# The head of a hybrid encoder block: memory loaded in halves, its norm behind the sixth K block, alternating heads, a pad of eight floats

## The chip, the cores and the metric

The kernel runs on one core of a Trainium2 chip, as one program. The metric is the device time of that program in microseconds: the median of several executions. One execution was also taken with the hardware profiler, and its span, from the first to the last instruction, is what the rows below are counted in.

## The reference, cut to what matters

One block of a streaming encoder on x of 512 frames by 1024 channels and a fixed memory of 256 frames by 1024 channels, all in float32. Three sub-layers with RMS norms ahead of them add to x: two recurrent branches that are merged, a cross-attention into the memory, and a gated convolution feed-forward. The change touches three places:

```python
def cross_attention(h, m, w_q, w_kv, w_o):      # m = rms_norm(mem, norm_mem_g)
    kv = m @ w_kv
    k = kv[..., :D_MODEL].reshape(bsz, -1, X_HEADS, X_HEAD_DIM)
    v = kv[..., D_MODEL:].reshape(bsz, -1, X_HEADS, X_HEAD_DIM)
...
def step(state, inp):                            # the first recurrence, 8 heads of 64
    r_t, w_t, k_t, v_t, a_t, b_t = inp
    sa = jnp.einsum('bhij,bhj->bhi', state, a_t)
    state = state * w_t[:, :, None, :] + sa[..., None] * b_t[:, :, None, :] + v_t[..., None] * k_t[:, :, None, :]
    y_t = jnp.einsum('bhij,bhj->bhi', state, r_t)
...
def conv_ffn(h, w_in, conv_w, conv_b, w_out):
    u = h @ w_in
    gate = causal_dwconv(u[..., :D_FF], conv_w, conv_b)
    return (jax.nn.gelu(gate) * u[..., D_FF:]) @ w_out
```

## The kernel before, in words

Every large product is computed as three products of float32r parts: a high part (a copy rounded by ScalarE) and a low part (the difference, by VectorE) of each operand, high by high, high by low, low by high (`mm3`, L163 to L167). `dense` does this for one block of 128 output channels over its blocks of the contraction. Weights come in pieces of 512 KB: the function `stream` loads a piece into one of four raw buffers (`wr`), ScalarE casts it into one of three buffers `wh` (L118), and VectorE subtracts into one of three buffers `wl` (L119). Loads, casts and subtractions have high priority. Each engine works through its own list in order; the order of these lists is laid out before the run by the framework, from the program's order, from priorities and from the times that it expects, so that products of a later part can stand between those of an earlier one. The framework also sets the semaphores.

The run begins with ten matmuls on a constant (`wake`, `NWAKE`). Then keys and values of the memory are computed. The memory is loaded in four quarters of 256 KB (`load_m`) that alternate with the two halves of w_k's first piece on the queue of SP; `split_m` scales one of its eight blocks by the norm's gain and splits it into high and low parts (`m2`). The RMS factor of each memory frame is not applied to the memory but to the results. For that, squares of the raw memory are taken on ScalarE behind the last split (L312, L315) and summed on VectorE (L316), then summed over partitions by TensorE (`rs_ps`, twice more with frames on partitions, `rmc_ps`), and turned into `rm` and `rmc` by Ln and Exp on ScalarE and a Newton step on VectorE (L250 to L254). In the program's order all of that stands ahead of K. The K product has eight blocks of 128 channels; block m needs piece m of w_k, has a PSUM bank of its own (`k_ps`), and is scaled by `rm` on VectorE (`kt`, L335) and written out by a transfer from the queue of POOL. From block 4 on, pieces of x are loaded. The V product follows: two halves of four pieces of w_v each, in PSUM tiles `v_ps`, and between them the sums and the normalisation of x (`x_norm`), which the projection `in_ps` needs.

The first recurrence is worked in eight chunks of 64 frames (`chunk`), at high priority between other matmuls. `rows_v(c)` transposes and centres the values of one chunk by 64x64 products: for each half e of the partitions and each of four pairs j of heads, one product reads the half e and writes the other half of one PSUM bank, 16 instructions in all. The products u read and write the same half; the second products into y (L843) do so too, both halves in one bank, and alternate between the halves.

The feed-forward uses a scheme of seven products (A11, s1, s2, s4, s3, A12, A22) for each pair of blocks of its 22; each has 24 matmuls of 256 columns in a pair, and the order is the one given here. Their moving operands are seven tiles: four in two tiles `hq` of the pool `big`, and three, those of s3, A12 and A22, in the tiles `hr0` to `hr2` of the pool `pr`, which is allocated from the right end of SBUF. The last product's operands `go1` and `go2` have 8 of their 11 blocks in `big` and 3 in the places of hr0 and hr1.

Of the kernel before, what the change touches and what calls it, by code (L numbers as in the profile page):

```python
# [9 lines left out]
F32 = mybir.dt.float32  # L10
F32R = mybir.dt.float32r
AF = mybir.ActivationFunctionType
ALU = mybir.AluOpType
# [4 lines left out]
P = 128  # L18
T = 512
D = 1024  # L20
KB = D // P
NMEM = 256
# [3 lines left out]
NPAIR = NH // 2  # L26
# [5 lines left out]
IN_REST = [22, 23, 24, 25, 26, 27, 28, 29, 30, 31, 32, 33, 34, 35, 36, 37, 14, 15, 16, 17, 18, 19, 20, 21]  # L32
NEARLY = 3
NMID = 10
NWAKE = 10
NPOOL = 2
KVB = 3
IN_ORDER = IN_RWKV + IN_REST
# [19 lines left out]
def hybrid_block_kernel(ctx: ExitStack, tc: tile.TileContext, xT_d, mT_d, pv_d, cst_d, win_d, wk_d, wv_d,  # L58
                        lup_d, gup_d, rga_d, rgx_d, wba_d, wbb_d, wmix_d, wq_d, wo_d, wfi_d, wfo_d, out_d):
    nc = tc.nc  # L60
    V, S, PE = nc.vector, nc.scalar, nc.tensor
# [12 lines left out]
    def mm_ps(name):  # L74
        return pmm.tile([P, T], F32, tag="mm", name=name)

    def rw_ps(name, pool=None, tag="rw", **kw):
        return (pool or prw).tile([P, T], F32, tag=tag, name=name, **kw)
# [15 lines left out]
        return pv[:, o:o + w]  # L94


    wdma, mdma = [], []

    def stream(dram, name, between=None, order=None):

        for g in order or range(dram.shape[0]):
            with tc.high_priority():
                raw = wp.tile([P, 1024], F32, tag="wr", name=f"{name}_r{g}", bufs=4)
                n = 1024 if between is None else 512
                for o in range(0, 1024, n):
                    ins = nc.sync.dma_start(raw[:, o:o + n], dram[g, :, o:o + n])
                    if between is not None:
                        tc.keep_in_program_order(ins)
                        between(o // n)
                    elif len(wdma) == 1:  # L110
                        tc.add_manual_dep(ins.ins, mdma[-1].ins.name, mybir.DependencyInfo(
                            mybir.DependencyClass.NoSync, mybir.DependencyReason.DATA), reason="order of the loads")
                between = None
                wdma.append(ins)
                hi = wp.tile([P, 1024], F32R, tag="wh", name=f"{name}_h{g}")
                lo = wp.tile([P, 1024], F32R, tag="wl", name=f"{name}_l{g}")
                for o in range(0, 1024, n):
                    S.copy(hi[:, o:o + n], raw[:, o:o + n])  # L118
                    V.tensor_tensor(lo[:, o:o + n], raw[:, o:o + n], hi[:, o:o + n].bitcast(F32), ALU.subtract)  # L119
            yield hi, lo  # L120

    def stream_quarters(srcs, name):
# [48 lines left out]
    def sum_behind(ins, n=1):  # L171

        for put in islice(sums, n):
            tc.add_manual_dep(tc.keep_in_program_order(put()).ins, ins.ins.name, mybir.DependencyInfo(
                mybir.DependencyClass.Sync, mybir.DependencyReason.DATA), reason="pace of the sums")

    def dense(ps, units, rhs, nkb, nsum=0):

        for kb in range(nkb):
            wh, wl = units.next()  # L180
            rh, rl = rhs(kb)
            ins = mm3(ps, wh, wl, rh, rl, kb == 0, kb == nkb - 1)
            if kb * nsum % nkb < nsum:
                sum_behind(ins)
        return ins
# [10 lines left out]
    eps = cp.tile([P, 4], F32, name="eps")  # L196
    ones = cp.tile([P, P], F32, name="ones")
# [13 lines left out]
    def rsqrt(out, src, scale, bias, load=True):  # L211

        if load:
            ins = ln_exp_set()
            with tc.issue_after(ins.ins):
                S.activation(out, src, AF.Ln, scale=scale, bias=bias)
                S.activation(out, out, AF.Exp, scale=-0.5)
        else:
            S.activation(out, src, AF.Ln, scale=scale, bias=bias)
            S.activation(out, out, AF.Exp, scale=-0.5)  # L220
# [27 lines left out]
    def newton(y, v, t, scale, bias):  # L248

        V.tensor_scalar(t, v, scale, bias, ALU.mult, ALU.add)  # L250
        V.tensor_tensor(t, t, y, ALU.mult)
        V.tensor_tensor(t, t, y, ALU.mult)
        V.tensor_scalar(t, t, -0.5, 1.5, ALU.mult, ALU.add)
        V.tensor_tensor(y, y, t, ALU.mult)  # L254

    def rstd_bc(out, ssq, n, pool=None, scratch=None, load=True, split=None, **kw):

        ps = rw_ps("rs_ps", pool, **kw)
        if split is None:
            PE.matmul(ps[:, :n], ones, ssq, start=True, stop=True)  # L260
        else:
            sum_exact(ps[:, :n], onesr, ssq, *split)
        rsqrt(out, ps[:, :n], 1.0 / D, eps[:, 0:1], load)
        if scratch is not None:
            newton(out, ps[:, :n], scratch, 1.0 / D, 1e-6)


    dK = dr.tile([KB, P, NMEM], F32, name="dK")
# [3 lines left out]
    with tc.tile_pool(name="p0", bufs=1, reuse_waits="tile") as p0:  # L272
# [6 lines left out]
        o = PV["nmem"][0]  # L279
        tc.keep_in_program_order(nc.scalar.dma_start(gm, pv_d[:, o:o + KB]))  # L280
        ln_exp_set()
        mraw = p0.tile([P, KB, NMEM], F32, name="mraw")
        xraw = p0.tile([P, KB, T], F32, name="xraw")

        def load_m(q):
            with tc.high_priority():
                mdma.append(tc.keep_in_program_order(
                    nc.sync.dma_start(mraw[:, 2 * q:2 * q + 2, :], mT_d[:, 2 * q:2 * q + 2, :])))

        load_m(0)  # L290
        m2 = p0.tile([P, 2, KB, NMEM], F32R, name="m2")

        def split_m(k):
            g = gm[:, k:k + 1]
            hi = S.activation(m2[:, 0, k, :], mraw[:, k, :], AF.Identity, scale=g)
            V.scalar_tensor_tensor(m2[:, 1, k, :], mraw[:, k, :], g, m2[:, 0, k, :].bitcast(F32),
                                   ALU.mult, ALU.subtract)
            return hi

        with tc.high_priority():  # L300
            for k in range(2):
                split_m(k)
        un = Units(wk_d, "wk")
        un.fill(lambda i: [load_m(q) for q in ((1,), (2, 3))[i]])
        tc.keep_in_program_order(nc.scalar.dma_start(pv, pv_d))
        mss = p0.tile([P, NMEM], F32, name="mss")
        msq = [p0.tile([P, NMEM], F32, tag="msq", name=f"msq{k}", bufs=2) for k in range(KB)]
        with tc.high_priority():
            for k in range(2, KB):
                last_m = split_m(k)  # L310
        with tc.issue_after(last_m.ins):
            S.activation(mss, mraw[:, 0, :], AF.Square)  # L312
        for k in range(1, KB):
            with tc.issue_after(last_m.ins):
                S.activation(msq[k], mraw[:, k, :], AF.Square)  # L315
            V.tensor_tensor(mss, mss, msq[k], ALU.add)  # L316
        rm = p0.tile([P, NMEM], F32, name="rm")
        rmt = p0.tile([P, NMEM], F32, name="rmt")
        rstd_bc(rm, mss, NMEM, scratch=rmt)
        rmc = p0.tile([P, 2], F32, name="rmc")  # L320
        psc = rw_ps("rmc_ps")
        for i in range(2):
            PE.matmul(psc[:, i:i + 1], mss[:, i * P:(i + 1) * P], ones[:, 0:1], start=True, stop=True)
        rsqrt(rmc, psc[:, 0:2], 1.0 / D, eps[:, 0:1], load=False)
        newton(rmc, psc[:, 0:2], rmt[:, 0:2], 1.0 / D, 1e-6)


        for m in range(KB):
            ps = rw_ps(f"k_ps{m}") if 3 <= m < 6 else mm_ps(f"k_ps{m}")
            dense(ps[:, :NMEM], un, lambda kb: (m2[:, 0, kb, :], m2[:, 1, kb, :]), KB)  # L330
            if m >= 4:
                with tc.issue_after(wdma[-1].ins):
                    nc.sync.dma_start(xraw[:, 2 * m - 8:2 * m - 6, :], xT_d[:, 2 * m - 8:2 * m - 6, :])
            kt = p0.tile([P, NMEM], F32, tag="kt", name=f"kt{m}", bufs=6)
            last_k = V.tensor_tensor(kt, ps[:, :NMEM], rm, ALU.mult)  # L335
            nc.gpsimd.dma_start(dK[m], kt)
        xss = p0.tile([P, T], F32, name="xss")
        for k in range(KB):
            if k == 0:
# [15 lines left out]
        for hf in range(2):  # L355
            pss = [(mm_ps if hf else rw_ps)(f"v_ps{hf}_{i}") for i in range(2)]
            for k2 in range(4):
                wh, wl = next(st)
                for kk in range(2):
                    kb = 2 * k2 + kk  # L360
# [170 lines left out]
    half = (slice(0, HD), slice(HD, P))  # L531
# [29 lines left out]
    for i in range(2):  # L561
        hs, oh = half[i], half[1 - i]
# [143 lines left out]
    with tc.tile_pool(name="pz", bufs=1, reuse_waits="tile") as pz:  # L706
# [9 lines left out]
        for s in range(30, -1, -1):  # L716
            n = 31 - s
# [66 lines left out]
    def rows_v(c):  # L784

        UV = ch.tile([P, 2, NPAIR, HD], F32, tag="UV", name=f"UV{c}", bufs=2)
        ps = ch_ps(f"vr{c}", "kv")
        for e in range(2):
            hs, oh = half[e], half[1 - e]
            for j in range(NPAIR):  # L790
                PE.matmul(ps[oh, j * HD:(j + 1) * HD], vT[hs, j, c * HD:(c + 1) * HD], centre[hs, hs],
                          start=True, stop=True)
        for e in range(2):
            oh = half[1 - e]
            S.copy(UV[oh, e], j3(ps[oh, 0:256]))
        return UV
# [322 lines left out]
    hq = [big.tile([P, 2, 2, 4, H], F32R, tag=f"act16_{i}", name=f"hq{i}") for i in range(2)]  # L1119
    hop = [hq[0][:, 0], hq[0][:, 1], hq[1][:, 0], hq[1][:, 1]]  # L1120
    hop += [pr.tile([P, 2, 4, H], F32R, tag=f"hr{i}", name=f"hr{i}") for i in range(3)]
    hop = dict(zip(("B11", "b1", "b2", "B22", "b3", "B21", "b4"), hop))
    ssf = cp.tile([P, T], F32, tag="ssq", name="ssf")

# [372 lines left out]
```

## Time and profile before

| | |
|---|---|
| median of 3 runs | 898.03 us (897.56 to 899.0) |
| the profiled execution, its own time | 896.3 us |
| its span, first to last instruction | 894.5 us |
| TensorE busy | 880.9 us, 98% of the span |
| VectorE, ScalarE busy | 686.6 us (77%), 514.8 us (58%) |
| mean granted TensorE clock | 0.997 |

The busy time of TensorE is the union of its instructions; matmuls overlap, so the spacing of their starts says more than the duration of one. Times in rows are in microseconds from the start of the span.

### The profile page before, as it was taken

How to read it: one execution, taken by the hardware profiler on the slowest of the kernel's cores; microseconds unless marked ns; L12 is line 12 of the kernel's file. 1: busy time of each engine (PE TensorE's matmuls, PEld its weight loads, DVE VectorE, ACT ScalarE, POOL GpSimd, SP SyncE). 2: the span in 40 equal slices, each digit the busy share in tenths (PEclk: the TensorE clock that was granted, in tenths of full speed). 3: DMA queues.
4: the chain of work that ended last, by engine and by line, in shares of the span. 5: the costliest groups of instructions: out<-in, count | busy, mean ns of one | idle time of the engine just before them, and what ended most of it. 6: DMA issues, size and time to landing. Idle time of an engine off the chain costs nothing.

```text
span 894.5 us, 15936 instructions
## 1 busy us (share of the span) xinstructions
PE 880.9 (98%) x6196; PEld 771.7 (86%) x6196; DVE 686.6 (77%) x1103; ACT 514.8 (58%) x782; POOL 132.6 (15%) x163
## 2 busy tenths in 40 slices
PE   8999999999999999999999999999999999999996
PEld 6978878888877777888887778999999999999996
DVE  6895598777967677675575578889889888999764
ACT  7665676634347676233554466756655566767553
POOL 0201222021102022001122111111111111202100
PEclk9999999999999999999999999999999999999998
DMA  8878799678987279758888958999989998998963
GB/s 277 292 258 218 202 223 241 184 206 230 266 220 155 73 201 234 230 161 234 217 235 185 196 139 187 256 262 284 260 256 309 256 305 245 259 276 203 282 196 94
DMA packets 97674, 201.37 MB, mean 225 GB/s; under 512 B 19584, under 2 KB 30976, under 8 KB 97536
## 3 DMA queue, kind: packets, MB, share of 16 engines
q1 hardware_dynamic: 62672, 118.57, 40.0%
q0 software_dynamic: 25504, 67.38, 37.0%
q10 hardware_dynamic: 9424, 14.42, 4.7%
q8 instruction: 48, 0.79, 0.4%
q14 instruction: 26, 0.21, 0.1%
HBM read 188.54 MB, written 78.12 MB: 298 GB/s over the span
## 4 chain that ended last, share of the span: by engine, by line
PE 92%; DVE 4%; ACT 1%; issue 1%; DMA 1%; SPq 0%; DVEq 0%; ACTq 0%
PE in_ps L165 7%; PE in_ps L166 7%; PE in_ps L164 7%; PE fx_ps L164 5%; PE fx_ps L165 5%; PE fx_ps L166 5%; PE fyz_ps L165 4%; PE fyz_ps L164 4%; PE fyz_ps L166 3%; PE ox_ps L166 2%; PE ox_ps L164 2%; PE ox_ps L165 2%; PE oyz_ps L166 2%; PE oyz_ps L165 2%; PE oyz_ps L164 2%; PE co_ps L165 2%
## 5 line engine op out<-in xcount | busy, mean ns | idle before, releaser
L130 ACT CAST wfi_h<-wfi_r 128x1024 fp32r<-128x1024 f32 x77 | 81.0, 1052 | 79.9 <-PE fx_ps L165 23.7
L164 PE MATMUL in_ps<-hT,win_h 128*128 128x512 f32 x304 | 120.6, 398 | 0.8 <-ACT hT L351 0.5
L166 PE MATMUL in_ps<-hT,win_l 128*128 128x512 f32 x304 | 121.0, 399 | 0.0
L165 PE MATMUL in_ps<-hT,win_h 128*128 128x512 f32 x304 | 120.9, 399 | 0.1
L131 DVE TENSOR_TENSOR wfi_l<-wfi_r,wfi_h 128x1024 fp32r<-128x1024 f32 x77 | 94.1, 1222 | 23.0 <-ACT wfi_h L130 22.7
L450 POOL DMA_DIRECT2D dS<-in_wfi x66 | 66.7, 1028 | 291.8 <-PE in_ps L164 109.1
L165 PEld LDWEIGHTS in_ps<-hT,win_h 128*128 128x128 f32 x304 | 57.1, 188 | 14.6 <-DVE hT L352 1.1
L164 PEld LDWEIGHTS in_ps<-hT,win_h 128*128 128x128 f32 x304 | 57.0, 188 | 14.3 <-ACT hT L351 1.0
L166 PEld LDWEIGHTS in_ps<-hT,win_l 128*128 128x128 f32 x304 | 57.1, 188 | 12.7 <-issue 0.7
L119 DVE TENSOR_TENSOR win_l<-win_r,win_h 128x1024 fp32r<-128x1024 f32 x38 | 46.3, 1221 | 28.1 <-ACT win_h L118 27.5
L486 POOL DMA_DIRECT2D dOs<-in_wfo x54 | 39.9, 795 | 180.2 <-PE fx_ps L164 50.0
L118 ACT CAST win_h<-win_r 128x1024 fp32r<-128x1024 f32 x38 | 39.9, 1049 | 39.5 <-PE in_ps L165 36.3
L1307 ACT CAST wfo_h<-wfo_r 128x1024 fp32r<-128x1024 f32 (+1 forms) x39 | 40.5, 1038 | 32.0 <-DMA wfo_r<-dOs 10.7
L1308 DVE TENSOR_TENSOR wfo_l<-wfo_r,wfo_h 128x1024 fp32r<-128x1024 f32 (+1 forms) x39 | 47.1, 1208 | 14.1 <-ACT wfo_h L1307 14.0
L164 PE MATMUL fx_ps<-hr,wfi_h 128*128 128x256 f32 x176 | 49.8, 283 | 0.0
L165 PE MATMUL fx_ps<-hr,wfi_h 128*128 128x256 f32 x176 | 49.7, 282 | 0.0
L166 PE MATMUL fx_ps<-hr,wfi_l 128*128 128x256 f32 x176 | 49.3, 280 | 0.0
L164 PE MATMUL fx_ps<-hq,wfi_h 128*128 128x256 f32 x176 | 49.3, 280 | 0.0
L166 PE MATMUL ox_ps<-go,wfo_l 128*128 128x256 f32 x176 | 49.3, 280 | 0.0
L164 PE MATMUL ox_ps<-go,wfo_h 128*128 128x256 f32 x176 | 49.3, 280 | 0.0
L165 PE MATMUL fyz_ps<-hq,wfi_h 128*128 128x256 f32 x176 | 49.3, 280 | 0.0
L165 PE MATMUL fx_ps<-hq,wfi_h 128*128 128x256 f32 x176 | 49.3, 280 | 0.0
(428 smaller groups left out, 2712.2 us busy)
## 6 DMA issues: line engine op xcount, KB each, us to landing
dS<-in_wfi POOLq DMA_DIRECT2D x66, 512.0 KB, 8.0
wfi_r<-dS SPq DMA_DIRECT2D x44, 512.0 KB, 6.5
win_r<-in_win SPq DMA_DIRECT2D x38, 512.0 KB, 5.2
wfi_r<-in_wfi SPq DMA_DIRECT2D x33, 512.0 KB, 5.3
dS<-dS POOLq DMA_DIRECT2D x22, 512.0 KB, 5.5
dOs<-in_wfo POOLq DMA_DIRECT2D x12, 512.0 KB, 8.0
wv_r<-in_wv SPq DMA_DIRECT2D x8, 512.0 KB, 4.9
dG<-gs ACTq DMA_DIRECT2D x16, 256.0 KB, 5.0
```

The source lines that it names most:

```text
L118: S.copy(hi[:, o:o + n], raw[:, o:o + n])
L119: V.tensor_tensor(lo[:, o:o + n], raw[:, o:o + n], hi[:, o:o + n].bitcast(F32), ALU.subtract)
L130: S.copy(hi, raw)
L131: V.tensor_tensor(lo, raw, hi.bitcast(F32), ALU.subtract)
L164: first = PE.matmul(ps, lh, rh, start=start, stop=False, **kw)
L165: PE.matmul(ps, lh, rl, start=False, stop=False, **kw)
L166: PE.matmul(ps, ll, rh, start=False, stop=stop, **kw)
L450: return lambda: nc.gpsimd.dma_start(s(out), src, **kw)
L486: yield lambda k=k, w=w, src=src: nc.gpsimd.dma_start(dO[n, m][:, k * P:(k + w) * P], src, **kw)
L1307: S.copy(hi[:, :n], raw[:, :n])
L1308: V.tensor_tensor(lo[:, :n], raw[:, :n], hi[:, :n].bitcast(F32), ALU.subtract)
```

## The change: what it does

It has three parts. The head of the kernel: the memory is loaded in two halves, w_k's first piece in one transfer between them; the first two pieces of w_k are cast and subtracted in halves; the fourth split of the memory stands between the halves of the first piece; block 1 takes its low products last; the squares stand behind the cast of w_k's third piece; the norm stands behind block 5, and so do the scalings of blocks 0 to 4; two blocks share a PSUM bank, so that six blocks wait for their scaling in three banks; there is an eleventh waking matmul. In `rows_v` the two loops change places. And the pool `pr` gets a fourth tile of eight floats (32 bytes) that nothing uses.

```diff
-NWAKE = 10
+NWAKE = 11
+KNORM = 5
...
                 raw = wp.tile([P, 1024], F32, tag="wr", name=f"{name}_r{g}", bufs=4)
-                n = 1024 if between is None else 512
-                for o in range(0, 1024, n):
-                    ins = nc.sync.dma_start(raw[:, o:o + n], dram[g, :, o:o + n])
...
+                n = 512 if len(wdma) < 2 else 1024
+                ins = nc.sync.dma_start(raw, dram[g])
+                if between is not None:
+                    tc.keep_in_program_order(ins)
+                    between(0)
...
                 for o in range(0, 1024, n):
-                    S.copy(hi[:, o:o + n], raw[:, o:o + n])
+                    casts.append(S.copy(hi[:, o:o + n], raw[:, o:o + n]))
                     V.tensor_tensor(lo[:, o:o + n], raw[:, o:o + n], hi[:, o:o + n].bitcast(F32), ALU.subtract)
+                    if between is not None and o == 0:
+                        between(1)
...
+    def dense_lo_last(ps, units, rhs, nkb):
+
+        w = [units.next() for _ in range(nkb)]
+        for kb in range(nkb):
+            for i in range(2):
+                PE.matmul(ps, w[kb][0], rhs(kb)[i], start=kb == i == 0, stop=False)
+        for kb in range(nkb):
+            PE.matmul(ps, w[kb][1], rhs(kb)[0], start=False, stop=kb == nkb - 1)
...
-                    nc.sync.dma_start(mraw[:, 2 * q:2 * q + 2, :], mT_d[:, 2 * q:2 * q + 2, :])))
+                    nc.sync.dma_start(mraw[:, 4 * q:4 * q + 4, :], mT_d[:, 4 * q:4 * q + 4, :])))
...
-            for k in range(2):
+            for k in range(3):
                 split_m(k)
         un = Units(wk_d, "wk")
-        un.fill(lambda i: [load_m(q) for q in ((1,), (2, 3))[i]])
+        un.fill(lambda i: load_m(1) if i == 0 else split_m(3))
...
+        def m_squares():
+            with tc.issue_after(casts[-1].ins):
+                S.activation(mss, mraw[:, 0, :], AF.Square)
...
+        def m_norm():
+            rstd_bc(rm, mss, NMEM, scratch=rmt)
...
+        def k_out(m):
+            kt = p0.tile([P, NMEM], F32, tag="kt", name=f"kt{m}", bufs=6)
+            ins = V.tensor_tensor(kt, k_ps[m], rm, ALU.mult)
+            nc.gpsimd.dma_start(dK[m], kt)
+            return ins

         for m in range(KB):
-            ps = rw_ps(f"k_ps{m}") if 3 <= m < 6 else mm_ps(f"k_ps{m}")
-            dense(ps[:, :NMEM], un, lambda kb: (m2[:, 0, kb, :], m2[:, 1, kb, :]), KB)
+            if m % 2 == 0:
+                ps2 = (rw_ps if m == 6 else mm_ps)(f"k_ps{m}")
+                k_ps += [ps2[:, :NMEM], ps2[:, NMEM:]]
+            (dense_lo_last if m == 1 else dense)(k_ps[m], un, lambda kb: (m2[:, 0, kb, :], m2[:, 1, kb, :]), KB)
...
+            if m == 2:
+                m_squares()
+            if m == KNORM:
+                m_norm()
+                for i in range(m):
+                    k_out(i)
+            if m >= KNORM:
+                last_k = k_out(m)
...
-        for e in range(2):
-            hs, oh = half[e], half[1 - e]
-            for j in range(NPAIR):
+        for j in range(NPAIR):
+            for e in range(2):
+                hs, oh = half[e], half[1 - e]
                 PE.matmul(ps[oh, j * HD:(j + 1) * HD], vT[hs, j, c * HD:(c + 1) * HD], centre[hs, hs],
                           start=True, stop=True)
...
     hop += [pr.tile([P, 2, 4, H], F32R, tag=f"hr{i}", name=f"hr{i}") for i in range(3)]
+    pr.tile([P, 8], F32, name="pad")
```

## Rows read from the trace of the kernel before

**Rows 1.** The page, first part: busy us, share, instructions of TensorE.
```profile
PE 880.9 (98%) x6196; PEld 771.7 (86%) x6196; DVE 686.6 (77%) x1103; ACT 514.8 (58%) x782; POOL 132.6 (15%) x163
```

**Rows 2.** Waits of TensorE, 5 to 70 us: total, times, longest.
```profile
PE k_ps L166 <- DVE wk_l L119: 1.0, 2, 0.8
...
PE rs_ps L260 <- DVE mss L316: 0.4, 1, 0.4
```

**Rows 3.** Stretches: length, busy of each engine, clock, DMA share, GB/s.
```profile
4.00:6.00 2.00, 2.00 (x7) 1.28 (x5) 1.19 (x3) 1.63 (x4) 0.00 (x0) 1.00 0.94 315
...
8.00:10.00 2.00, 1.28 (x7) 1.00 (x7) 1.26 (x3) 1.82 (x5) 0.00 (x0) 1.00 1.02 412
```

**Rows 4.** Instructions of the memory's tile mraw, durations in ns; its landings.
```profile
L315 ACT ACTIVATE msq<-mraw x7: 400/418/420, 10.2 to 16.8; 128x256 f32<-128x256 f32 x7
...
DMA to landing us min/median/max: 3.3/4.7/6.0
```

**Rows 5.** Timeline of the first microseconds: start, length, engine, line, operation.
```profile
0.75 0.40 SPq L288 DMA_DIRECT2D mraw<-in_mT  x1
...
1.33 4.51 PE L277 MATMUL wake<-onesr 128*128 128x512 f32 x10 [1.33 <-DVE Pp L584]
...
4.24 0.91 ACT L295 ACTIVATE m<-mraw,gm 128x256 fp32r<-128x256 f32 x2 [1.76 <-DMA gm<-in_pv]
...
5.06 0.60 ACT L118 CAST wk_h<-wk_r 128x512 fp32r<-128x512 f32 x1
5.69 0.69 DVE L119 TENSOR_TENSOR wk_l<-wk_r,wk_h 128x512 fp32r<-128x512 f32 x1
...
5.71 0.38 PE L164 MATMUL k_ps<-m,wk_h 128*128 128x256 f32 x1
```

**Rows 6.** Timeline of TensorE, end of block 2 to the start of V.
```profile
17.73 0.28 PE L166 MATMUL k_ps<-m,wk_l 128*128 128x256 f32 x1
...
18.07 0.28 PE L166 MATMUL k_ps<-m,wk_l 128*128 128x256 f32 x1
18.78 0.70 PE L260 MATMUL rs_ps<-mss,ones 128*128 128x256 f32 x2 [0.43 <-DVE mss L316]
...
19.68 0.37 PE L164 MATMUL k_ps<-m,wk_h 128*128 128x256 f32 x1
...
33.90 0.39 PE L164 MATMUL v_ps<-wv_h,m 128*128 128x512 f32 x1
34.13 0.39 PE L165 MATMUL v_ps<-wv_l,m 128*128 128x512 f32 x1
```

**Rows 7.** Timeline of VectorE: a subtraction of w_k, the fifth scaling of K.
```profile
23.75 1.23 DVE L119 TENSOR_TENSOR wk_l<-wk_r,wk_h 128x1024 fp32r<-128x1024 f32 x1 [0.25 <-ACT wk_h L118]
...
26.17 0.42 DVE L335 TENSOR_TENSOR kt<-k_ps,rm 128x256 f32<-128x256 f32 x1
```

**Rows 8.** Stretch of 50 to 60 us: VectorE is the third number behind the length.
```profile
50.00:60.00 10.00, 9.68 (x42) 7.47 (x40) 10.00 (x14) 7.43 (x11) 0.00 (x0) 1.00 0.81 249
```

**Rows 9.** Timeline of the chunk stage: y, u, rows_v (vr), what follows, and a copy.
```profile
281.36 0.68 PE L843 MATMUL y<-BZ,UV 64*64 64x64 f32 x16
...
284.59 0.51 PE L829 MATMUL u<-Xs,BZ 64*64 64x64 f32 x10
...
285.78 0.51 PE L165 MATMUL in_ps<-hT,win_h 128*128 128x512 f32 x1
...
285.94 0.74 ACT L795 COPY UV<-vr 64x256 f32<-64x256 f32 x2 [0.27 <-PE vr L791]
...
289.64 0.96 PE L791 MATMUL vr<-cst,vT 64*64 64x64 f32 x16
```

**Rows 10.** Timeline of TensorE in the feed-forward: first matmuls of A11, s3, A11.
```profile
635.44 0.28 PE L164 MATMUL fx_ps<-hq,wfi_h 128*128 128x256 f32 x1
...
646.75 0.28 PE L164 MATMUL fx_ps<-hr,wfi_h 128*128 128x256 f32 x1
...
655.39 0.28 PE L164 MATMUL fx_ps<-hq,wfi_h 128*128 128x256 f32 x1
```

More of the change, by code (lines that the diff above doesn't have):

```diff
@@ L94, in parall @@
         return pv[:, o:o + w]
-    wdma, mdma = [], []
+    wdma, mdma, casts = [], [], []
     def stream(dram, name, between=None, order=None):
@@ L103, in stream @@
                 raw = wp.tile([P, 1024], F32, tag="wr", name=f"{name}_r{g}", bufs=4)
-                n = 1024 if between is None else 512
-                for o in range(0, 1024, n):
-                    ins = nc.sync.dma_start(raw[:, o:o + n], dram[g, :, o:o + n])
[L107 to L113, printed above, removed]
+                n = 512 if len(wdma) < 2 else 1024
[3 more added lines that the diff above has]
+                    between(0)
+                elif len(wdma) == 1:
+                    tc.add_manual_dep(ins.ins, mdma[-1].ins.name, mybir.DependencyInfo(
+                        mybir.DependencyClass.NoSync, mybir.DependencyReason.DATA), reason="order of the loads")
                 wdma.append(ins)
@@ L117, in stream @@
                 for o in range(0, 1024, n):
-                    S.copy(hi[:, o:o + n], raw[:, o:o + n])
+                    casts.append(S.copy(hi[:, o:o + n], raw[:, o:o + n]))
                     V.tensor_tensor(lo[:, o:o + n], raw[:, o:o + n], hi[:, o:o + n].bitcast(F32), ALU.subtract)
+                    if between is not None and o == 0:
+                        between(1)
+                between = None
             yield hi, lo
@@ L308, in hybrid_block_kernel @@
         with tc.high_priority():
-            for k in range(2, KB):
+            for k in range(4, KB):
                 last_m = split_m(k)
[L311 to L316, printed above, removed]
+        def m_squares():
+            with tc.issue_after(casts[-1].ins):
+                S.activation(mss, mraw[:, 0, :], AF.Square)
+            for k in range(1, KB):
+                with tc.issue_after(casts[-1].ins):
+                    S.activation(msq[k], mraw[:, k, :], AF.Square)
+                V.tensor_tensor(mss, mss, msq[k], ALU.add)
@@ L317, in hybrid_block_kernel @@
         rm = p0.tile([P, NMEM], F32, name="rm")
         rmt = p0.tile([P, NMEM], F32, name="rmt")
-        rstd_bc(rm, mss, NMEM, scratch=rmt)
         rmc = p0.tile([P, 2], F32, name="rmc")
[L321 to L325, printed above, removed]
+        def m_norm():
+            rstd_bc(rm, mss, NMEM, scratch=rmt)
+            psc = rw_ps("rmc_ps")
+            for i in range(2):
+                PE.matmul(psc[:, i:i + 1], mss[:, i * P:(i + 1) * P], ones[:, 0:1], start=True, stop=True)
+            rsqrt(rmc, psc[:, 0:2], 1.0 / D, eps[:, 0:1], load=False)
+            newton(rmc, psc[:, 0:2], rmt[:, 0:2], 1.0 / D, 1e-6)
@@ L328, in hybrid_block_kernel @@
+        k_ps = []
+        last_k = None
+        def k_out(m):
[3 more added lines that the diff above has]
+            return ins
         for m in range(KB):
-            ps = rw_ps(f"k_ps{m}") if 3 <= m < 6 else mm_ps(f"k_ps{m}")
-            dense(ps[:, :NMEM], un, lambda kb: (m2[:, 0, kb, :], m2[:, 1, kb, :]), KB)
+            if m % 2 == 0:
+                ps2 = (rw_ps if m == 6 else mm_ps)(f"k_ps{m}")
+                k_ps += [ps2[:, :NMEM], ps2[:, NMEM:]]
+            (dense_lo_last if m == 1 else dense)(k_ps[m], un, lambda kb: (m2[:, 0, kb, :], m2[:, 1, kb, :]), KB)
@@ L333, in hybrid_block_kernel @@
                     nc.sync.dma_start(xraw[:, 2 * m - 8:2 * m - 6, :], xT_d[:, 2 * m - 8:2 * m - 6, :])
-            kt = p0.tile([P, NMEM], F32, tag="kt", name=f"kt{m}", bufs=6)
-            last_k = V.tensor_tensor(kt, ps[:, :NMEM], rm, ALU.mult)
-            nc.gpsimd.dma_start(dK[m], kt)
+            if m == 2:
[6 more added lines that the diff above has]
+                last_k = k_out(m)
         xss = p0.tile([P, T], F32, name="xss")
```

## The prediction

> **What bounds the kernel now.** The page's first part shows TensorE busy for 98% of the span [rows 1], so an edit counts only where it shortens TensorE's own work or removes a wait of it. The waits of TensorE from 5 to 70 us come next: five rows, 3.1 us together, of which the first and the last are shown, four of them in the K product [rows 2]. The timeline gives the length of that stretch: the first product of K starts at 5.71 us, the first of V at 33.90, 28.19 us for 192 matmuls and the sums of the memory's norm [rows 5, 6]. From 19.68 to 33.90 the last 120 run at 118 ns each [rows 6], so 192 would need 22.7 us; with 0.9 us for the sums some 4.6 us of the stretch are waits or gaps. The rows that group time by stretch say why it starts slowly: at 4 to 6 us the queue moved 315 GB/s in 2 KB rows, at 8 to 10 us 412 GB/s in 4 KB rows [rows 3]. In the chunk stage and the feed-forward products no wait of TensorE is listed; there one reads the spacing of the matmuls.
>
> **First part: the head of the K product.** Before, the first quarter of the memory, issued at 0.75, landed 3.3 us later, at 4.05 [rows 4, 5]. A half is twice the bytes; 256 KB more at 412 GB/s are 0.64 us, so it lands between 4.05 and 4.7; I take 4.7. Each 512 KB behind it takes 1.27 us [rows 3]: w_k's first piece at 6.0, the second half of the memory at 7.2, w_k's second piece at 8.5 and its third at 9.8. Before, the last quarter came 6.0 us after its issue, past 9 us [rows 4], with w_k's second piece behind it, so the new order brings them about 2 us sooner. The price is the start: cast to first matmul was 0.65 us [rows 5], so it moves from 5.71 to 6.65. The eleventh waking matmul (0.45 us, a tenth of the ten [rows 5]) ends at 6.3 and hides in that; without that cover it would cost its 0.45 us. The short idle stretch that follows should not cost the clock: from 8 to 10 us TensorE is idle for 0.72 of 2.00 us at a granted clock of 1.00, the level of 2.4 GHz [rows 3].
>
> Then the chain on ScalarE and VectorE. Two splits take 0.91 us on ScalarE, some 0.41 us apart, and I give VectorE as much [rows 5]; a half piece of w_k takes 0.60 and 0.69 us. Laid end to end: three splits, half cast, fourth split, half cast, four splits on ScalarE from 4.7 to 9.15; VectorE follows to 9.95. The last products of block 0 end at 10.3. Block 1 has its low products last, and finds its halves cast at 9.7 and 10.2 and subtracted at 10.6 and 11.2, so it runs through: 24 matmuls at 113 ns (the spacing before 18.07) end at 13.0. Before, block 2 ended at 18.18 and block 1 thus at 15.5: 2.5 us are won. The squares behind the third cast are 8 x 0.42 us on ScalarE [rows 4], beside one cast of two times 0.60 us per block of 2.7 us; with their 7 short sums on VectorE they fit before block 5 ends. The sums of the norm, then long ready, cost 0.9 us of TensorE and no longer the 1.5 us between 18.18 and 19.68 [rows 6]: 0.6 us more. As far as this goes the K product wins 3.0 us, and would end at 30.9.
>
> **The new wait.** All scalings by the norm now stand behind block 5: those of blocks 0 to 4, that of block 5, and behind block 6's product its own, ahead of block 7, which writes the other half of block 6's bank. No row shows a matmul that waits for a reader of the other half of its bank. The nearest row is ScalarE's copy of one half of the rows_v bank at 285.94: it sat idle 0.27 us until the last matmul into the other half was done [rows 9]. So I take it that block 7 waits for block 6's scaling. The Trainium skill, PSUM — Partial Sum Buffer, section PSUM bank collisions raise a hardware error, says that TensorE may not write a bank and partition group while VectorE reads it; by that rule too block 7 must wait, and without the rule the sum would have the whole 3.0 us.
>
> When is that scaling done? Block 5 ends at 13.0 plus four blocks, 24.2 with blocks between 2.72 and 2.84 us. Before, from the start of the norm's sums at 18.78 to the end of the fifth scaling at 26.59 were 7.8 us, two 1.2 us subtractions among them [rows 6, 7]; two more scalings at 0.41 give 8.6, so 32.8. Without those subtractions it is 30.3. Block 6 ends at 27.9 (24.2, 0.9 for the sums, 2.8). TensorE then has up to 4.9 us in which block 7 can't run. V's products can stand there if the order on TensorE puts them there: pieces 0 and 1 of w_v are 24 matmuls of 0.233 us [rows 6], 5.6 us. But the buffers of piece 2 are those of w_k's last piece, free when block 7 is done at 35.6; the cast (two halves of 0.60 [rows 5]) and the subtraction (1.23 [rows 7]) take 2.4 us; TensorE has 0.7 us of V left, so it waits 1.7 us. The start then wins 3.0 - 1.7 = 1.3. Bounds: 3.0 if block 7 is ready by 31, and a loss of 1.7 (35.6 against 33.90) if V doesn't fill in. Behind this VectorE is full from 50 to 60 [rows 8]; I hold that it starts as much earlier as V does.
>
> **Second part: rows_v.** The 64x64 products of one head half, then of the other, become pairs that alternate. Alone, 16 instructions take 0.96 us busy; the product of the states (L843), which alternates, takes 0.68 for 16 [rows 9]. Behind the u products, u and rows_v together last from 284.59 to 285.78, 1.19 us; there the first products of rows_v overlap the last u already, so of the 0.28 I count 0.23. Twice 0.28 and six times 0.23 are 1.9 us at most; nothing at least, where the step behind waits for VectorE. No wait of TensorE is listed in the stage, so I take 1.6. The Trainium skill, TensorEngine Tiling (Array Packing), section Gotcha 1: PSUM Pressure, says that different row tiles cannot write one PSUM bank at the same time; by it rows_v, one bank for both halves, would win 0. The L843 row disagrees: its halves too go to one bank, at the alternating pace.
>
> **Third part: the pad.** Eight floats behind hr0 to hr2 push the right-hand pool down by 32 bytes. The trace prints no addresses, but it shows what differs: from 635.44 to 646.75 four products read hq, 96 matmuls at 117.8 ns; from 646.75 to 655.39 three read hr, 72 at 120.0 [rows 10]. If the address is the cause, 2.2 x 72 x 11 pairs of blocks is 1.75 us, and the part of go1 and go2 that lies in the same pool adds some 48 products of three at about 4 ns: 0.2. Sum 1.9 on TensorE's own path; nothing if the cause is another.
>
> **The rivals.** (a) *Block 7 is ready in time*: VectorE takes no subtraction between, scaling ends at 30.3, and all of 3.0 + 1.6 + 1.9 = 6.5 stays: 891.5. For it, the rows without the two subtractions give just that; against it, w_v's subtractions have the higher priority, as w_k's had. (b) *The wait takes the place of the one removed*: V does not fill in, 1.7 is lost at the start, 3.5 won later: 896.2. For it, the order on an engine is laid down before the run. (c) *rows_v gains nothing*: the pairs run one behind the other in their bank, and the 0.96 stays: 1.3 + 1.9, 894.8. (d) *The pad does not act*, because the spacing of hr comes from elsewhere: 1.3 + 1.6, 895.1. (e) *Slower*: the same scaling of block 6, with block 7 alone behind it, is pushed back by the subtractions and x's sums. Each us of it is a us of TensorE; it outweighs the 3.5 of the other parts, and the 0.2%, once it ends past 36.4 (36.4 + 2.8 - 33.9 = 5.3). Before, the sixth and seventh scalings came with such gaps, but there they waited for their products. At 38 it is 901.4.
>
> **How the numbers follow.** The profiled execution took 896.3 with a span of 894.5; the median of the three runs is 898.03, 1.7 above it, and the difference is carried over. Forecast: 1.3 + 1.6 + 1.9 = 4.8, 891.5 for such an execution and 893.2 for the median. Chances: forecast 0.40 (its own range 892 to 895), (a) 0.20, (b) 0.17, (c) 0.08, (d) 0.08, (e) 0.07. About 0.2%, 1.8 us, is what a measurement can tell here. Faster by more: the forecast, (a), (c), (d) and half of (b), 0.84; within: the other half, 0.09; slower 0.07. The range 890.6 to 896.8 leaves out (e), the top of (b) and the lower tail of (a).
>
> **What would show it.** First K product near 6.65, block 1 through by 13; no wait of rs_ps for the squares' sum; V's first product before K's last; the stretch between block 6 and block 7, and what ended it; 16 rows_v instructions in about 0.68; hr's products at 117.8. The prediction fails if the half lands much past 4.7, if block 7 stands idle for several us, or if the order of the chunk stage, laid out anew, loses what rows_v gives.

## The result, and the profile after

| | before | changed |
|---|---|---|
| median of 5 executions each, same chip | 898.44 us | 893.38 us (891.61 to 894.56) |
| ratio, 95% interval | | 0.9945 (0.993 to 0.996) |
| the profiled execution: its own time, span | 896.3, 894.5 us | 894.56, 892.8 us |

The kernel is 5.1 us faster (3.6 to 6.3). The two profiled executions lie only 1.7 us apart: that of before was below all its timed ones, that of the changed kernel was its slowest. So what follows goes by stages, and by more than one profile.

The page's first part, against [rows 1]: TensorE is busy 3.5 us less, and the share is the same.
```profile
PE 877.4 (98%) x6197; PEld 767.9 (86%) x6197; DVE 685.2 (77%) x1104; ACT 513.6 (58%) x783; POOL 132.5 (15%) x163
```
The head. Timeline of the first microseconds, against [rows 5]:
```profile
0.75 0.40 SPq L299 DMA_DIRECT2D mraw<-in_mT  x1
...
1.33 4.45 PE L288 MATMUL wake<-onesr 128*128 128x512 f32 x11 [1.33 <-DVE Pp L616]
...
5.80 1.30 ACT L306 ACTIVATE m<-mraw,gm 128x256 fp32r<-128x256 f32 x3 [3.31 <-DMA gm<-in_pv]
...
7.01 0.49 ACT L306 ACTIVATE m<-mraw,gm 128x256 fp32r<-128x256 f32 x1
7.41 1.12 ACT L117 CAST wk_h<-wk_r 128x512 fp32r<-128x512 f32 x2
...
8.07 0.39 PE L166 MATMUL k_ps<-m,wk_h 128*128 128x256 f32 x1 [2.29 <-ACT wk_h L117]
```
The landings of the memory's halves, against [rows 4]:
```profile
DMA to landing us min/median/max: 4.9/5.7/6.5
```
The first half landed 4.9 us after its issue, at 5.65; four splits stand ahead of the first cast, and K starts at 8.07. Stretches, against [rows 3] (the third number from the end is the granted clock, the last GB/s):
```profile
2.00:4.00 2.00, 2.00 (x6) 1.57 (x5) 0.00 (x0) 0.49 (x1) 0.00 (x0) 1.00 0.68 200
4.00:6.00 2.00, 1.78 (x6) 1.04 (x4) 0.00 (x0) 0.20 (x1) 0.00 (x0) 1.00 0.99 361
6.00:8.00 2.00, 0.00 (x0) 0.00 (x0) 1.66 (x4) 2.00 (x6) 0.00 (x0) 1.00 1.03 418
8.00:10.00 2.00, 1.81 (x7) 1.50 (x8) 1.98 (x5) 2.00 (x6) 0.00 (x0) 0.58 1.03 422
10.00:12.00 2.00, 2.00 (x13) 2.00 (x12) 2.00 (x5) 2.00 (x4) 0.00 (x0) 0.57 1.03 401
```
TensorE stood idle from 5.78 to 8.07, and from 8 to 12 us the granted clock is 0.58 and 0.57, so for most of these 4 us at the lower level, 1.2 of 2.4 GHz. From 9.18 to 11.73 the 12 products of K are 213 ns apart, then 118: 1.1 us lost. Waits of TensorE from 5 to 70 us, against [rows 2]:
```profile
PE k_ps L166 <- ACT wk_h L117: 2.3, 1, 2.3
PE k_ps L166 <- DVE kt L348: 0.8, 1, 0.8
PE in_ps L167 <- DVE hT L384: 0.2, 1, 0.2
```
The wait for the sum of squares is gone; one for a scaled K block (`kt`) is new. Timeline of TensorE, against [rows 6]:
```profile
26.93 0.59 PE L271 MATMUL rs_ps<-mss,ones 128*128 128x256 f32 x2
...
27.72 0.37 PE L166 MATMUL k_ps<-m,wk_h 128*128 128x256 f32 x1
...
30.64 0.39 PE L166 MATMUL v_ps<-wv_h,m 128*128 128x512 f32 x1
...
41.88 0.38 PE L166 MATMUL k_ps<-m,wk_h 128*128 128x256 f32 x1 [0.81 <-DVE kt L348]
...
44.81 0.40 PE L168 MATMUL v_ps<-wv_h,m 128*128 128x512 f32 x1
```
Block 6 runs from 27.72, 44 products of V from 30.64, and block 7 only at 41.88. Why so late stands on VectorE's timeline, against [rows 7]:
```profile
38.73 1.08 DVE L348 TENSOR_TENSOR kt<-k_ps,rm 128x256 f32<-128x256 f32 x3
41.40 0.42 DVE L348 TENSOR_TENSOR kt<-k_ps,rm 128x256 f32<-128x256 f32 x1 [1.59 <-DMA dK<-kt]
```
Block 6's scaling has no buffer: there are six (`bufs=6`), and the first is still read by its transfer, which began at 36.7. VectorE stands 1.59 us, with w_v's next subtraction behind it, and TensorE 0.8.

A mark for what the head is worth: the first product of the tile `bo` stands behind it, near 195 us, ahead of all that the other two parts touch. Its first row, before and then changed:
```profile
L624 PE MATMUL bo<-bhi,bonesr x1: 389/389/389, 195.0 to 195.0; 128*128 128x512 f32 x1
```
```profile
L656 PE MATMUL bo<-bhi,bonesr x1: 389/389/389, 195.1 to 195.1; 128*128 128x512 f32 x1
```
In this pair of profiles the head has won nothing. The stretch of the chunk stage, instructions of `vr` alone, before and then changed:
```profile
273.00:330.00 57.00, 7.70 (x128) 6.60 (x128) 5.86 (x16) 1.00 0.58 129
```
```profile
273.00:330.00 57.00, 5.45 (x128) 4.35 (x128) 5.88 (x16) 1.00 0.60 141
```
TensorE works 2.25 us less on rows_v, and where it stands alone it takes 0.68 us, not the 0.96 of [rows 9]. The start of the next stage behind the chunks (`yb`) is 1.36 us closer to the mark than it was before the change. First matmuls of A11, s3, A11 in the feed-forward, against [rows 10]:
```profile
633.95 0.28 PE L166 MATMUL fx_ps<-hq,wfi_h 128*128 128x256 f32 x1
...
645.26 0.28 PE L166 MATMUL fx_ps<-hr,wfi_h 128*128 128x256 f32 x1
...
653.74 0.28 PE L166 MATMUL fx_ps<-hq,wfi_h 128*128 128x256 f32 x1
```
96 products of hq in 11.31 us and 72 of hr in 8.48: both 117.8 ns, where hr had 120.0.

### The profile page after: what moved, and what is told of

Same layout as the page of the kernel before. It is cut to its first block, busy times and chain, and to the rows that moved or that the text cites. A ratio compares the mean times of both kernels' runs of the same rounds, so it can differ in the third digit from the quotient of the medians.

```text
span 892.8 us, 15934 instructions
## 1 busy us (share of the span) xinstructions
PE 877.4 (98%) x6197; PEld 767.9 (86%) x6197; DVE 685.2 (77%) x1104; ACT 513.6 (58%) x783; POOL 132.5 (15%) x163
## 4 chain that ended last, share of the span: by engine, by line
PE 91%; DVE 4%; DMA 2%; ACT 1%; issue 1%; DVEq 0%; ACTq 0%; SPq 0%
PE in_ps L167 7%; PE in_ps L166 7%; PE in_ps L168 7%; PE fx_ps L167 5%; PE fx_ps L166 5%; PE fx_ps L168 5%; PE fyz_ps L167 4%; PE fyz_ps L166 4%; PE fyz_ps L168 3%; PE ox_ps L166 2%; PE oyz_ps L166 2%; PE ox_ps L168 2%; PE oyz_ps L168 2%; PE oyz_ps L167 2%; PE ox_ps L167 2%; PE co_ps L167 2%
## 5 line engine op out<-in xcount | busy, mean ns | idle before, releaser
L118 DVE TENSOR_TENSOR win_l<-win_r,win_h 128x1024 fp32r<-128x1024 f32 x38 | 46.3, 1221 | 24.2 <-ACT win_h L117 20.7
L166 PE MATMUL fyz_ps<-hq,wfi_h 128*128 128x256 f32 x176 | 49.2, 280 | 0.0
L167 PE MATMUL fyz_ps<-hq,wfi_h 128*128 128x256 f32 x176 | 49.2, 280 | 0.0
```

The source lines that it names most:

```text
L166: first = PE.matmul(ps, lh, rh, start=start, stop=False, **kw)
L167: PE.matmul(ps, lh, rl, start=False, stop=False, **kw)
```

## The experiments

Theories. **1**: the three parts add up, each near its size in the prediction. **2**: the head gives nothing, and the other two parts and the spread make the 5 us. Rivals for single steps: **3**, in a single part the reason is another (the spacing of hr hangs on something else than the address; the step behind rows_v waits anyway); **A**, the head's gain is lost at block 7's wait and VectorE's wait for the transfer; **B**, VectorE's work as a whole sets when the input projection runs freely; **C**, it is lost to the clock; **D**, the clock falls by chance. The table has for each kernel the ratio of its median to that of before on the same chip, and from its profile the span, the start of `bo` (behind the head), what is left behind it, and the two-microsecond stretches of the head with a granted clock under 0.9.

| kernel | ratio (95%) | span | `bo` | behind it | clock under 0.9 |
|---|---|---|---|---|---|
| before | 1 | 894.5 | 195.0 | 699.5 | none |
| changed | 0.9945 (0.993 to 0.996) | 892.8 | 195.1 | 697.7 | 8 to 12 |
| e1_pad | 0.9968 (0.9958 to 0.9979) | 892.6 | 197.0 | 695.6 | 10 to 18 |
| e2_rows | 0.9982 (0.997 to 0.9995) | 892.8 | 194.4 | 698.4 | none |
| e3_head | 0.9997 (0.9983 to 1.0011) | 894.8 | 194.7 | 700.1 | none |
| e4_pad_rows | 0.9959 (0.9943 to 0.9975) | 890.9 | 196.0 | 694.9 | 10 to 14 |
| e5_kt8 | 0.9953 (0.9938 to 0.9968) | 892.6 | 194.1 | 698.5 | 8 to 12 |
| e8_banks | 0.9955 (0.9939 to 0.9971) | 896.5 | 194.4 | 702.1 | 10 to 14 |
| e9_kt8_banks | 0.9955 (0.994 to 0.997) | 887.8 | 193.9 | 693.9 | 8 to 12 |
| e10_kt8_banks_wake | 0.9951 (0.9938 to 0.9965) | 889.4 | 192.4 | 697.0 | none |
| f1_wake20 | 0.9952 (0.9937 to 0.9966) | 890.6 | 193.4 | 697.2 | none |
| f2_pad64 | 0.9967 (0.9953 to 0.9981) | 895.1 | 198.5 | 696.6 | 12 to 20 |
| f3_whole | 0.9953 (0.9935 to 0.997) | 894.0 | 194.9 | 699.1 | 10 to 14 |
| f4_kt8_banks_wake18 | 0.9954 (0.994 to 0.9967) | 891.0 | 193.6 | 697.4 | none |

**e1_pad.** The kernel before, and
```diff
+    pr.tile([P, 8], F32, name="pad")
```


> The kernel before with the eight floats behind hr0 to hr2 alone. Theory 1 (the three parts add up, each near its size in the prediction): hr's products fall from 120.0 to 117.8 ns, 72 matmuls in 11 pairs of blocks and the part of go1 and go2 in that pool, 1.9 us faster. Theory 2 (the two later parts are smaller, and most of the 5 us between the medians comes from the head or from the spread of executions): in the changed kernel's trace the feed-forward's first products win 1.5 us from 554.7 to 774.9, so 1.5 at most. Theory 3 (the spacing of hr hangs on something else that changed with it): 0, and 120.0 ns stays. The head's rows stay as they were in each.

Measured 2.9 us faster (1.9 to 3.8), more than any theory said; theory 1's 1.9 is at the edge of the interval. The spacing of hr is that of hq throughout, but both change together: from 612 to 699 us it is 113.3 ns, elsewhere 117.8. The row of that stretch, and of a later one:
```profile
640.00:680.00 40.00, 40.00 (x355) 40.00 (x354) 38.18 (x54) 26.32 (x40) 6.55 (x9) 1.00 0.93 269
704.00:742.00 38.00, 38.00 (x323) 37.82 (x322) 31.94 (x45) 21.03 (x31) 6.18 (x9) 1.00 0.96 279
```
355 products in 40 us and 323 in 38, at the same granted clock of 1.00. And the head, which is that of before, lost its clock:
```profile
12.00:14.00 2.00, 1.49 (x6) 0.90 (x5) 1.49 (x3) 2.00 (x4) 0.00 (x0) 0.50 0.56 224
14.00:16.00 2.00, 2.00 (x10) 2.00 (x11) 1.90 (x4) 1.83 (x4) 0.00 (x0) 0.50 0.56 109
```

**e2_rows.** The kernel before, with the loops of rows_v exchanged.
```diff
-        for e in range(2):
-            hs, oh = half[e], half[1 - e]
-            for j in range(NPAIR):
+        for j in range(NPAIR):
+            for e in range(2):
+                hs, oh = half[e], half[1 - e]
```


> The kernel before with the two loops of rows_v exchanged alone. Theory 1: 16 instructions in 0.68 us instead of 0.96, and 1.6 us faster. Theory 2: the stage from 274 to 330 us wins 1.3 to 1.4, as in the changed kernel's trace. Theory 3 (the step behind waits for the copies anyway): the instructions take 0.68 and the time stays within 0.5 us.

1.6 us faster (0.4 to 2.7). In the timeline the product takes 0.68 us:
```profile
288.08 0.68 PE L791 MATMUL vr<-cst,vT 64*64 64x64 f32 x16
```
The stage from 274 to 330 wins 1.4. Theories 1 and 2 both hold here; theory 3, less than 0.5 us, does not.

**e3_head.** The changed kernel without the pad and with rows_v as before.

> The changed kernel without the pad and with rows_v as before: the head alone. Theory 1: 1.3 to 1.6 us faster than before (the 5.06 between the medians less 1.9 and 1.6). Theory 2 (what the changed kernel's trace shows: TensorE stands idle from 5.8 to 8.07 us, the granted clock is 0.58 at 8 to 12 us, and block 7 stands behind V, so that the input projection is no sooner than before at 111 us): 0, between 0.5 faster and 0.5 slower. In both the first product of K starts near 8.1, and the wait of a K block for a scaling stays.

0.3 us faster, anything from 1.5 faster to 1.0 slower: nearer to theory 2, with theory 1's 1.3 not excluded. This execution kept its clock (1.00 from 6 to 12 us, K without a gap from 8.88), and still its mark is only 0.3 earlier: the 44 V products between blocks 6 and 7 stand for 1.1 us in several gaps while VectorE is behind with w_v, then comes the wait for `kt` (0.7).

**e4_pad_rows.** The kernel before, with pad and exchanged loops.

> The kernel before with the pad and the exchanged loops, the head as before. Theory 1: 3.5 us faster than before, and 1.3 to 1.6 slower than the changed kernel on its chip. Theory 2 (the head gives nothing): as fast as the changed kernel, both by what pad and loops give, 2.9 to 5.0. If the head costs something, this kernel is the fastest of the four.

3.7 us faster (2.2 to 5.1): theory 1's size for the two. The changed kernel's medians are 0.5 to 1.3 us better than that on their chips, less than the intervals tell apart.

**e5_kt8, e8_banks, e9_kt8_banks.** The changed kernel with eight `kt` buffers; with a bank of its own for block 7; with both.
```diff
-            kt = p0.tile([P, NMEM], F32, tag="kt", name=f"kt{m}", bufs=6)
+            kt = p0.tile([P, NMEM], F32, tag="kt", name=f"kt{m}", bufs=8)
...
-                k_ps += [ps2[:, :NMEM], ps2[:, NMEM:]]
+                ps3 = rw_ps("k_ps7") if m == 6 else ps2
+                k_ps += [ps2[:, :NMEM], ps3[:, NMEM:]]
```


> The changed kernel with eight buffers for the scaled K blocks instead of six. In the traces of the changed kernel and of the head alone, the seventh scaling waits 1.6 us for a transfer that still reads the first scaled block's buffer, and ends at 41.8 us; block 7 waits for it behind 41 products of V. Theory A (that wait is where the head's gain went): the scaling is done by 40.3, the 0.7 to 0.8 us wait of block 7 goes, VectorE's later work starts 1.6 sooner, and the kernel is 0.8 to 1.6 faster than the changed one, 6 to 6.7 faster than before. Theory B (VectorE's work as a whole sets when the input projection runs at full pace, near 66 us): its work is the same, so it is within 0.5 of the changed kernel. Theory C (the loss is TensorE's clock, which fell in some executions): within 0.5 as well, and the spread between executions stays.

> The changed kernel with a bank of its own for block 7. Theory A (the shared bank costs the head its gain): block 7 runs directly behind block 6, V starts some 2.8 us later than in the changed kernel but has three weight buffers and no waits inside; V ends at 54.8 instead of 57 us; 1 to 2 us faster than the changed kernel. Theory B (VectorE's work as a whole decides): V ends sooner, the input projection's first products then wait for the normalised x, and at 70 us nothing is left; within 0.5 of the changed kernel. The seventh scaling's wait for its buffer is still there, so VectorE stands as before.

> The changed kernel with both: eight buffers for the scaled blocks and a bank of its own for block 7. Theory A: no wait of TensorE between the end of block 0 and the input projection, and VectorE never stands for a transfer: 1.5 to 2.5 us faster than the changed kernel, 6.5 to 7.5 faster than before. Theory B: within 0.5 of the changed kernel, with the waits moved to the input projection's first products.

The marks move as theory A has it and not B (no more than 0.5), with a fallen clock in each: 195.1, then 194.1, 194.4 and 193.9, one profile each. In the waits of TensorE from 5 to 70 us of the kernel with both nothing is left behind the first microseconds:
```profile
PE k_ps L166 <- ACT wk_h L117: 2.0, 1, 2.0
PE k_ps L168 <- DVE wk_l L118: 0.2, 1, 0.2
```
With a bank of its own block 7 runs directly behind block 6, without a wait. But the medians stay at 4.0 to 4.2 us faster than before. A gain of 0.7 to 1.2 can't be seen in them, and what theory A forecast for the whole kernel of e5 and e9, 6 to 7.5 faster than before, lies outside their intervals (2.7 to 5.6): a miss. Part of the spread is in the rows: e8's profile lost 3.4 us in the attention, where ScalarE waits 3.09 us for a reload of K. Waits of TensorE there:
```profile
PE prT_ps L1122 <- DVE ex L1120: 2.5, 1, 2.5
```
The changed kernel has this wait too, 0.65 us in its first profile and 2.40 in f3, and e5 has 1.79; TensorE lost 0.3, 2.0 and 1.9 in that stage. In the six profiles without the whole change, and in e9, e10, f1 and f4, ScalarE waits 0.15 us at most there. Whether the change brings it about, and so takes back what the head gains, no run here tells.

**e10_kt8_banks_wake, f1_wake20, f4_kt8_banks_wake18.** With both and 20 waking matmuls; the changed kernel with 20 alone; with both and 18.

> The same with 20 waking matmuls instead of 11, so that TensorE works until the first product of K can start near 8 us. Theory C (the idle stretch from 5.8 to 8.1 us is what lets the clock fall, as in the changed kernel's trace, and the 17 products at 213 instead of 118 ns cost 1.6 us in such executions): granted clock 1.00 from 8 us on in the profile, spread between executions smaller than the 3 us of the changed kernel, and up to 1.6 faster than the same kernel with 11. Theory D (the clock falls for other reasons, or what it costs is made up before 66 us): within 0.3 of the same kernel with 11. If the data come early, the added waking matmuls cost up to 0.3.

> The changed kernel with 20 waking matmuls, nothing else: TensorE works until the first product of K can start. Theory C (the idle stretch from 5.8 to about 8 us lets the clock fall: among the profiles with that stretch four of five show a granted clock of 0.5 over some 3.4 us, and with 20 waking matmuls the one profile there is shows none): no product of K at 213 ns behind 8 us, and at 111 us the kernel is 1.0 to 1.6 us ahead of the changed kernel's profile. Theory D (the clock fell by chance): 213 ns products behind 9 us here too, and no more than 0.5 ahead. In the medians either may be hidden, since executions of one kernel lie 3 to 7 us apart.

> Eight buffers for the scaled blocks, a bank of its own for block 7 and 18 waking matmuls: the head with its three losses taken out, and the waking matmuls cut so that they end where the first product of K starts. Theory A and C (the losses were the clock, block 7's wait and VectorE's wait for a transfer): at 111 us 2.6 us ahead of the kernel before, and in the median 1 to 2.5 faster than the changed kernel. Theory B (VectorE's work as a whole decides): at 111 us no more than 1 ahead of before, the same median as the changed kernel.

Theory C: none of the three shows a fallen clock. Stretches of f1:
```profile
6.00:8.00 2.00, 1.52 (x8) 0.92 (x7) 1.82 (x5) 2.00 (x6) 0.00 (x0) 1.00 1.04 424
8.00:10.00 2.00, 2.00 (x15) 1.88 (x16) 2.00 (x5) 2.00 (x6) 0.00 (x0) 1.00 1.02 416
```
Its mark, 193.4, is 1.5 and 1.6 us ahead of the changed kernel's two; e10's, 192.4, is 1.5 ahead of e9's. In f4 a new wait of 1.4 us (V's bank, for the norm's chain on VectorE) takes 1.2 of it back. In the medians (4.1 to 4.4 us faster than before) again nothing can be told; the 1 to 2.5 ahead of the changed kernel that A and C forecast for f4 did not come. So no version is shown to beat the changed kernel, though e10's head ends 2.7 us sooner.

**f2_pad64.** The kernel before, with a pad of sixteen floats, 64 bytes.

> The kernel before with a pad of sixteen floats instead of eight: the pool moves by 64 bytes, so the address of hr0 to hr2 keeps its remainder by 64. Theory 1 (the remainder by 64 bytes decides): hr's products stay at 120.0 ns, no stretch of 113.3 ns spacing outlives one of them, and the time is that of before within 0.8 us. Theory 3 (the pad acts by something else, as another place of the whole pool): 117.8 ns and 2 to 3 us faster, as with eight floats.

A miss for both: the spacing goes with theory 1, the time with 3. hr stays slower than hq by what the address would have it: first matmuls of s3, A11, s3, A11 on its timeline:
```profile
650.45 0.28 PE L164 MATMUL fx_ps<-hr,wfi_h 128*128 128x256 f32 x1
...
659.08 0.28 PE L164 MATMUL fx_ps<-hq,wfi_h 128*128 128x256 f32 x1
...
669.97 0.28 PE L164 MATMUL fx_ps<-hr,wfi_h 128*128 128x256 f32 x1
...
678.38 0.28 PE L164 MATMUL fx_ps<-hq,wfi_h 128*128 128x256 f32 x1
```
72 of hr in 8.63 us are 119.9 ns; then 96 of hq in 10.89 are 113.4 and 72 of hr in 8.41 are 116.8. Yet the kernel is 3.0 us faster (1.7 to 4.2), as with eight floats, and its lowest execution, 892.52, is 3.5 below the lowest of 72 of before, 896.04. What its profile has and that of before has not is the closer spacing, in the last six of eleven pairs of blocks: 6 x (96 x 4.4 + 72 x 3.1 ns) = 3.9 us. From the first product of A11 to the start of the last product it takes 216.7 us, before took 220.3.

**f3_whole.** The changed kernel again, on the last chip.

> The changed kernel as it is, on the same chip as the three others. Theory 1 of the whole (the head gives 1.3): 4.8 faster than before here too. Theory 2 (the head gives nothing or little): 4.0 to 5.0, no more than 1 ahead of what pad and loops gave alone (3.7). The granted clock falls at 8 to 12 us or does not, and in its rows one sees which.

4.2 us faster than before (2.7 to 5.8), clock fallen, mark at 194.9.

## Why the time came out as predicted

The total was right, 893.2 for 893.38; two of its three terms were not right for the reasons given. That it came out within 0.2 us is luck: measured alone, the head gave 0.3 for 1.3, rows_v 1.6 for 1.6 and the pad 2.9 for 1.9, and the two errors cancel.

**The start of K.** Failed. The half was to land at 4.7 and landed at 5.65: the term "256 KB more at 412 GB/s" took the rate of a queue that had been running for 8 us; at 4 to 6 us the changed kernel moved 361 GB/s, at 2 to 4 us 200. Memory and w_k come in rows of 4 KB there, so the slow start is not one of 2 KB rows alone, as the prediction read it. A fourth split ahead of the first cast is 0.4 more. K began at 8.07, not 6.65, and block 6 ended at 30.64, not 27.9: 1.4 of these 2.7 us are the late start, 1.1 the 12 products at 213 ns.

**"The short idle stretch should not cost the clock."** Failed. It was read from a stretch that held 0.72 us of idleness; here there were 2.3 in one piece. Where TensorE waited for its first cast for 1.6, 1.7, 2.0, 2.2 and 2.3 us the clock fell (e8, f3, e9, e5, changed), at 1.5 it did not (e3), and with 18 or 20 waking matmuls it did not. e8 and e3 waited nearly alike (1.57 and 1.54), so the length of the wait alone does not say whether it falls. By the marks of f1 and e10 against their pairs a fall costs about 1.5 us; but e3, which kept its clock, was only 0.3 to 0.4 ahead of f3 and the changed kernel, with 1.1 lost among V's products.

**The head of before was taken from one good execution.** Its clock falls too: not in the profiles of before and e2, but in e1, e4 and f2, where products of K wait 1.0 to 1.9 us for a split of the memory. The five marks of that head are 194.4 to 198.5, mean 196.2; the three of the new head with six buffers and eleven waking matmuls (changed, e3, f3) 194.7 to 195.1, mean 194.9. The difference, 1.3, is the predicted size, by luck, since the reason is another: the new head hardly beats the old one at its best, and lacks its bad executions. Five and three profiles are few, and e3's median (0.3, interval from 1.5 faster) neither shows nor excludes 1.3.

**Sums of the norm.** Right: no wait, 0.8 us for them (26.93 to 27.72).

**Block 7.** That it waits for block 6's scaling is shown (the `kt` wait, and e8 and e9, where a bank of its own takes it away). That agrees with the Trainium skill, PSUM — Partial Sum Buffer, section PSUM bank collisions raise a hardware error, in so far as the wait is there (0.8 us); it is a semaphore's, and what the chip would do without it no run shows. V filled in, so rival (b) is out, and with more products than thought: pieces 2 and 3 of w_v did not need w_k's last buffer (they were subtracted at 34.72 and 37.52, ahead of block 7), so 44 products ran, not 24. The scaling was to be done at 32.8 and was at 41.8: block 5 ended 2.7 us late (26.93 for 24.2), the norm's chain and the scalings shared VectorE with the sums of x and with four subtractions of w_v, not two, and the six buffers were overlooked; they cost 1.59 us on VectorE. Rivals (a) and (e) stay out, the first by these rows. The scaling was later than the 36.4 from which (e) would have made the kernel slower; it did not, because V's products stood ahead of block 7 and only 0.8 us came through to TensorE.

**rows_v.** Right in instruction (0.68 us) and size (1.6 alone, 1.4 in the stage); rival (c) is out. The starts show how: products of one half follow each other in 58 ns in both kernels, and in the changed one each has a product of the other half 7 ns behind it. The rule of the Trainium skill, TensorEngine Tiling (Array Packing), section Gotcha 1: PSUM Pressure, would have given 0; these rows speak against it for products that alternate between two row halves and write the two partition halves of one bank.

**The pad.** The mechanism as far as it went is right: 117.8 ns with 32 bytes, 119.9 with 64; that the address is what counts is argued from these two pads, since the trace prints none. The size of this term is right too: with what starts lie more than 130 ns apart taken off, the feed-forward's first products are 1.7 us shorter than before in each of the five profiles with the small pad and no closer stretch among them (changed, e4, e8, e10, f3). The gain of the pad as a whole was mis-sized: 2.9 for 1.9, and f2 has 3.0 with hr still 2.1 to 3.4 ns behind hq. Both pads come with stretches at 113.3 ns. Behind 550 us such a stretch of over 10 us stands in 9 of the 11 profiles with a pad and in none of the 3 without (before, e2, e3; in e2 one of 2.8 us ended with the first products of hr). So part of the pad's gain is this, which the sum did not have. Why a pad of either size lets it last is open; no run here tells it.

## What to carry to other kernels

A forecast from one profile takes over the luck of that execution: a stage that waits at the start of a run should be seen in several before its gain is priced. When results wait in fewer banks for a late factor, count the buffers behind the scaling as well as the banks. And where a larger first transfer makes the first product wait, fill that wait with waking matmuls: in three profiles the clock then stayed up, and two of the marks were 1.5 us sooner, though the medians could not show it.

## What the runs showed of the hardware

- 256-column matmuls of float32r that read hq ran 117.8 or 113.3 ns apart, at a granted clock of 1.00; the closer spacing lasted up to 87 us (e1). In most cases the spacing changed at a gap of 0.05 to 1 us, in f2 (659 us) without one.
- With no pad or one of 64 bytes, matmuls that read hr were 2.1 to 2.2 ns slower than those of hq at the one spacing and 3.4 at the other (f2); with a pad of 32 bytes they were not.
- Matmuls of 64x64 that read one half of the partitions and write the other started mostly 58 ns apart in the order by half; alternating, two of them, one of each half, started 7 ns apart and the pairs 58 ns.
- The clock can fall after TensorE is back at work: in e8 the products of K are 113 ns apart from 8.9 to 9.9 us, behind the idle stretch, and 213 to 218 from 10.1 to 13.3.
